# A hybrid attention and gMLP encoder block on one Trainium2 core: squares by tokens, normalisation on VectorE, one-matmul gate scales, mixes of two query tiles in one run, and a re-laid order of steps

## The chip, the cores and the metric

The kernel runs on one core of a Trainium2 chip. The metric is the device time in microseconds (us) of one execution. The engines are TensorE (PE, with its weight loads shown apart as PEld), VectorE (DVE), ScalarE (ACT), GpSimd (POOL) and SyncE (SP). SP's queue issues nearly all DMAs, ACT's queue a few.

## The reference

One pre-norm layer over 1024 tokens of width 1024, then a final RMSNorm. Cut to what matters:

```python
h = rmsnorm(x, norm_gain)
z = h @ w_in                       # 1024 x 4864, split into eight parts
q, k, v, gate_a, u_in, v_in, gate_b, g_merge = split(z)
q, k = axial_rope(rmsnorm(q, q_gain)), axial_rope(rmsnorm(k, k_gain))
attn = softmax(q k' / 8) v * silu(gate_a)        # 8 query heads, 2 key heads of 64
y_a  = attn @ w_proj_attn
vv   = layernorm(gelu(v_in)), mixed by a 128 x 128 matrix per channel group inside chunks of 128 tokens
gm   = gelu(u_in) * (w_spatial vv + b_spatial) * silu(gate_b)
y_b  = gm @ w_proj_gmlp
g    = sigmoid(g_merge + b_merge)                # two gates of width 1024
out  = rmsnorm(x + (g0 * y_a + g1 * y_b) @ w_out, final_gain)
```

## The kernel before, in words

Nearly every product is made three times, as high times high, high times low and low times high part (`mm3`, L187 to L190, and `z_mm`, L568 to L573), in fp32r or fp16. Splitting an operand takes one ACT instruction for the high part and one DVE instruction for the low part (`split16`, L301 to L303; `split`, L122 to L124).

The work goes in stages, and a scheduler keeps roughly to the order in which the program lists the steps (L964 to L1298, written out by hand, with dependences, buffer rings and a few `high_priority` blocks):

1. **Load stage.** x arrives transposed (`xT`, eight tiles of 128 channels x 1024 tokens, `load_x`, L158) with the k/v weights and the v_in weights (`nat_weight`, tile `wraw`, ring of 4). PE makes k and v (tile `kv`) and the first v_in group (tile `v`, `v_group`, L474). For the RMS of each token, `add_square` squares each x tile on ACT (L178, six tiles) or POOL (L176, two tiles), DVE adds the eight squares up (L182), and eight one-column matmuls (L265, tile `sst`) sum over channels. `power_rstd` (L138 to L140; the power is on POOL) makes `rstd`. Eight matmuls (L280, tile `rb`) and two DVE copies (L283) lay it out along the free axis as `rB`.
2. **Norm stage.** `v_group(1)` to `v_group(3)` run on PE; each ends in two Gelu instructions on ACT that empty its bank (L481, tile `vst`). x is read again as four pairs of tiles (`load_pair`, L310, tile `xp`). `norm_part` (L312) multiplies each tile with `rB`: tiles 0, 1 and 3 on DVE (L315), tiles 2, 4, 5, 6 and 7 on POOL as two halves each (L318). `norm_split` (L322) scales and splits them into the fp16 tiles `x16`, on ACT (L302) and DVE (L303). `scales` reads the q weights and four more blocks on ACT's queue (tiles `sqq`, `squ`, ...) for unit scales, and `prep_q` (L508) loads, scales and splits the eight q weight halves (tiles `wraw`, `wq`). `v_post` and `spatial` are the gMLP token mix (tile `sp`), and `bias_term` (L495) its bias: one 512-column matmul with ones and four DVE instructions on 64 rows each.
3. **q stage.** `q_group(0)` to `q_group(3)` on PE (tile `q`), between them `spatial`, key transposes, and the query chain `q_norm`, `q_split` that ends in transposed queries `qT`.
4. **Attention.** 64 `scores` steps (L632), one for each head of a pair, query tile and pair of heads j: four score matmuls, row maximum on DVE (L640), exponential on ACT (L644), the normalised fp16 high part on ACT (L650) and low part on DVE (L651), then a DMA transpose on SP's queue into tile `T` (L654, ring `ptr` of 2). 32 `mix` steps (L656) multiply a transposed tile with v: 48 small matmuls into the one bank `o`, and an ACT copy of 128 columns (L667). 24 fills (`run_fill`, gates and u, 24 matmuls each into the one bank `z`) lie between them, with their weights from `prep_next`.
5. **After attention.** `proj_b` (tile `yb`), eight gate pairs (tile `g`), `proj_a` (tile `y`), the output product (tile `out`) and the final norm. Each gate pair takes a unit scale from `unit_scale` (L287): four matmuls of one column that add up in PSUM (L292, tile `usg`), an ACT copy (L294) and four POOL instructions.

PSUM has three banks of 1024 columns in ring `S` (for `kv`, `v`, `sp`, `q`, `s` and the later stages) and one of 512 each for `o` and `z`. So a `q_group` can start only when an earlier tile in its bank has been emptied.

Of the kernel before, what the change touches and what calls it, by code (L numbers as in the profile page):

```python
# [30 lines left out]
def hybrid_block_kernel(  # L31
# [60 lines left out]
    def C(c):  # L92
        return slice(128 * c, 128 * c + 128)
# [17 lines left out]
    ones = t2("ones")[:, 0:P]  # L111
    dve.memset(ones, 1.0)

# [38 lines left out]
    def load_x(dt):  # L152
        raw = t4("T16", f"xraw{dt}")
        t = tX(f"xhl{dt}")
        hi, lo = t[:, 0, :], t[:, 1, :]
        cuts = [slice(0, 256), slice(256, 512), H(1)] if dt == 0 else [H(0), H(1)] if dt < 3 else [slice(0, 1024)]
        for i, r in enumerate(cuts):
            nc.sync.dma_start(out=raw[:, r], in_=xT[C(dt), r])  # L158
            if dt == 0 and i == 0:
                nc.scalar.dma_start(out=cs, in_=cst[:, 0:C_BSP])  # L160
            if dt == 0 and i != 1:
                first_w(i // 2)
        for r in cuts:
# [5 lines left out]
        xraw0.append(raw)  # L169

    ssq = []

    def add_square(dt):
        t = t4("xa", f"xsq{dt}")
        if dt in SQPOOL:
            pool.tensor_tensor(out=t, in0=xraw0[dt], in1=xraw0[dt], op=ALU.mult)  # L176
        else:
            act.activation(t, xraw0[dt], AF.Square)  # L178
        if dt == 0:
            ssq.append(t)  # L180
        else:
            (pool if dt in ADPOOL else dve).tensor_tensor(out=ssq[0], in0=ssq[0], in1=t, op=ALU.add)  # L182

    xraw0 = []
    SQPOOL, ADPOOL = (1, 4), ()
# [20 lines left out]
    for i in range(4):  # L206
        for j in range(2):
# [49 lines left out]
    dve.tensor_scalar(out=gsc[:, 0:1], in0=ssp[:, 16:17], scalar1=2.0 ** -16, scalar2=1e-30, op0=ALU.mult, op1=ALU.add)  # L257
# [4 lines left out]
    sst = ps_o("sst")  # L262
    for tt in range(NT):
        with tc.high_priority():
            pe.matmul(sst[:, tt:tt + 1], ssq[0][:, C(tt)], ones[:, 0:1], start=(tt == 0), stop=(tt == NT - 1))  # L265
    power_rstd(rstd, sst[:, 0:NT], NT, 1.0 / D)
# [20 lines left out]
    def unit_scale(ss, n, name, tag="sc", bufs=3):  # L287
# [3 lines left out]
        for i in range(n):  # L291
            pe.matmul(pt[:, 0:1], mscale.broadcast_to([P, P]), ss[:, i:i + 1], start=(i == 0), stop=(i == n - 1))  # L292
        sc = sb.tile([P, 2], F32, tag=tag, bufs=bufs, name=f"sc{name}")
        act.copy(sc[:, 1:2], pt[:, 0:1])  # L294
# [10 lines left out]
    x16, xpair = {}, {}  # L305
# [14 lines left out]
    NPD = (0, 1, 3)  # L320

    def norm_split(dt):  # L322
        raw = xpair[dt // 2][:, dt % 2, :]
        if dt < 4:
            t = sb.tile([P, 2, 1024], F16, tag="xa", bufs=BUFS["xa"], name=f"x16{dt}")
        else:
            if dt % 2 == 0:
                x16["t"] = tX16(f"x16{dt}")
            t = x16["t"][:, dt % 2]
        split16(t[:, 0, :], t[:, 1, :], raw, gs[:, dt:dt + 1], "dve")  # L330
        x16[dt] = t
# [163 lines left out]
    def bias_term(h):  # L495
        pt = ps_o(f"wsum{h}")
        pe.matmul(pt, ones, wsr[h], start=True, stop=True)
        for t in (2 * h, 2 * h + 1):
            for g2 in range(2):
                rows = slice(64 * g2, 64 * g2 + 64)  # L500
                dve.scalar_tensor_tensor(
                    out=bsp[rows, C(t)], in0=pt[rows, C(2 * (t % 2) + g2)], scalar=cs[rows, C_LNB + t:C_LNB + t + 1],
                    in1=bsp[rows, C(t)], op0=ALU.mult, op1=ALU.add)
# [128 lines left out]
    def scores(j, qt, h):  # L632
# [331 lines left out]
    v_group(0)  # L964
    bsp = t2("bsp")
# [18 lines left out]
    load_wsp(0)  # L984
    early = scales(["q"] + order[:4], ["xa"] * 8)
# [3 lines left out]
    load_pair(0)  # L989
    norm_part(3)  # L990
    v_group(1)
    ktmp = t4("vS", "ktmp")
    head_norm(kn, ktmp, 0, 8, "kf")
    v_group(2)
# [5 lines left out]
    rope(kn, ktmp, Ak, Bk, 8, 2)  # L1000
    norm_part(0)
    norm_split(0)
    norm_part(1)
# [7 lines left out]
    norm_split(1)  # L1011
    v_group(3)
    norm_part(5)
    bias_term(0)
    with tc.high_priority():
# [14 lines left out]
        dve.tensor_scalar(out=vsc, in0=vsc, scalar1=1.0 / (PSCALE * VSCALE), scalar2=None, op0=ALU.mult)  # L1030
    v_post(0)
    spatial(0)
    v_post(1)
    spatial(1)
    bias_term(1)
    norm_split(3)
    prep_q(0)
    prep_q(1)
    prep_q(2)
    prep_q(3)  # L1040
    dve.tensor_tensor(out=v3, in0=v3, in1=vinv[:, None, :].broadcast_to([P, 8, 128]), op=ALU.mult)
# [19 lines left out]
    norm_split(7)  # L1061
    kT = [tX(f"kT{v}") for v in range(2)]
    khl = tX("khl")
    khl = [khl[:, 0, :], khl[:, 1, :]]
    split(khl[0], khl[1], kn, act)
    q_group(0)
    v_post(3)
    spatial(2)
    qT = [t8("qT", 4, f"qT{j}") for j in range(4)]
    k_transposes(0)  # L1070
    v_post(4)
    k_transposes(1)
    q_norm(0)
    v_post(5)
    k_transposes(2)
    spatial(3)
    scales(order[4:6])
    k_transposes(3)
    q_group(1)
    spatial(5)  # L1080
    prep_next()
    spatial(4)
    q_group(2)
    q_split(0)
    prep_next()
    q_split(1)
    v_post(6)
    spatial(6)
    scales(order[6:8])
    v_post(7)  # L1090
    q_norm(1)
    prep_next()
    q_split(2)
    spatial(7)
    q_group(3)
    prep_next()
    q_split(3)
    v_affine(1)
    v_affine(0)
    scores(*hs[0])  # L1100
    prep_next()
    v_affine(3)
    prep_next()
    scales(order[10:12])
    scores(*hs[1])
    scores(*hs[2])
    scales(order[8:10])
    scores(*hs[3])
    v_affine(2)
    run_fill(*halves[0])  # L1110
    prep_next()
    scores(*hs[4])
    q_norm(2)
    run_fill(*halves[1])
    q_split(5)
    scores(*hs[5])
    scores(*hs[6])
    mix(*hs[0][:2])
    q_split(4)
    scores(*hs[7])  # L1120
    mix(*hs[2][:2])
    scores(*hs[8])
    scores(*hs[9])
    q_norm(3)
    scores(*hs[10])
    scores(*hs[11])
    q_split(6)
    q_split(7)
    mix(*hs[4][:2])
    scores(*hs[12])  # L1130
    scores(*hs[13])
    mix(*hs[6][:2])
    run_fill(*halves[2])
    mix(*hs[8][:2])
    scores(*hs[14])
    scores(*hs[15])
    scores(*hs[16])
    mix(*hs[10][:2])
    scores(*hs[17])
    scores(*hs[18])  # L1140
    mix(*hs[12][:2])
    scores(*hs[19])
    mix(*hs[14][:2])
    run_fill(*halves[3])
    run_fill(*halves[4])
    prep_next()
    prep_next()
    run_fill(*halves[5])
    run_fill(*halves[6])
    scores(*hs[20])  # L1150
    run_fill(*halves[7])
    scores(*hs[21])
    scores(*hs[22])
    mix(*hs[16][:2])
    mix(*hs[18][:2])
    run_fill(*halves[8])
    scores(*hs[23])
    scores(*hs[24])
    prep_next()
    scores(*hs[25])  # L1160
    scores(*hs[26])
    mix(*hs[20][:2])
    run_fill(*halves[9])
    prep_next()
    scores(*hs[27])
    scores(*hs[28])
    scores(*hs[29])
    run_fill(*halves[10])
    mix(*hs[22][:2])
    scores(*hs[30])  # L1170
    mix(*hs[24][:2])
# [3 lines left out]
    run_fill(*halves[11])  # L1175
    scores(*hs[34])
    run_fill(*halves[12])
    mix(*hs[26][:2])
    scores(*hs[35])
    mix(*hs[28][:2])  # L1180
    scores(*hs[36])
    prep_next()
    scores(*hs[37])
    scores(*hs[38])
    mix(*hs[30][:2])
    run_fill(*halves[13])
# [91 lines left out]
    gate(6)  # L1278
    pws[7] = pair_weights(7)
# [3 lines left out]
    split_y(0)  # L1283
# [112 lines left out]
```

## Time and profile before

| | us |
|---|---|
| median of 3 runs | 746.68 |
| lowest and highest | 745.58, 747.12 |
| the profiled execution | 748.41 |
| its span in the trace | 746.6 |
| PE busy in the span | 713.0 (95%) |
| DVE busy | 591.8 (79%) |
| ACT busy | 452.6 (61%) |
| POOL busy | 132.3 (18%) |

A matmul of 512 columns has a duration of about 0.38 to 0.40 us in the trace, but the next one starts some 0.22 us after it, because matmuls overlap. So PE's time is read here from the starts of its matmuls, and its busy share only tells where it stood idle. Times within the span are counted from the span's start.

### The profile page before, as it was taken

What the parts mean: (1) busy time and instruction counts of PE and PEld (TensorE: products, weight loads), DVE (VectorE), ACT (ScalarE), POOL (GpSimd) and SP (SyncE); (2) the same over time, 40 slices, a digit from 0 to 9 for tenths busy, and PEclk for the clock granted to TensorE, in tenths of its full rate; (3) what the DMA queues carried; (4) which work ended last, traced back from release to release, by engine and by line L of the source; (5) the groups of instructions that cost most, each with busy time, mean ns of one, the idle gap of its engine ahead of it and who ended that gap; (6) DMA issues with size and microseconds to landing.
All of it is one profiled execution on the core that took longest, in us unless ns stands there. A gap on an engine that the chain in (4) does not pass through costs nothing.

```text
span 746.6 us, 12013 instructions
## 1 busy us (share of the span) xinstructions
PE 713.0 (95%) x4685; PEld 471.2 (63%) x4685; DVE 591.8 (79%) x824; ACT 452.6 (61%) x808; POOL 132.3 (18%) x118
## 2 busy tenths in 40 slices
PE   7989879889999999999999999999999999999996
PEld 7978636455556555666656787556464466478885
DVE  7859989879989999777977699889687898972323
ACT  8563468887688898677785477655463445531011
POOL 3027731332301020001110025202002010000000
PEclk9999979999999999999999999999999999999999
DMA  8690144437487996998889921130031013330202
GB/s 309 224 356 7 57 140 155 129 113 141 88 176 144 205 196 114 160 164 141 156 150 219 270 85 45 41 127 16 1 141 57 1 56 128 135 137 26 110 32 84
DMA packets 156360, 93.98 MB, mean 126 GB/s; under 512 B 135824, under 2 KB 136464, under 8 KB 156304
## 3 DMA queue, kind: packets, MB, share of 16 engines
q1 hardware_dynamic: 154864, 88.75, 47.4%
q10 hardware_dynamic: 1440, 4.47, 1.7%
q8 instruction: 36, 0.59, 0.3%
q14 instruction: 20, 0.16, 0.1%
HBM read 55.46 MB, written 4.19 MB: 80 GB/s over the span
## 4 chain that ended last, share of the span: by engine, by line
PE 47%; DVE 20%; DMA 11%; ACT 10%; issue 7%; POOL 4%; SPq 1%; POOLq 0%; DVEq 0%; ACTq 0%
DMA T<-p 5%; PE out L189 4%; PE out L190 4%; PE out L188 4%; DVE p L651 4%; DVE nm L640 3%; PE g L188 3%; PE g L190 3%; PE g L189 3%; ACT p L650 2%; DMA sqq<-in_wall_dram 2%; DMA xraw<-in_xT_dram 2%; ACT P L644 2%; PE o L663 1%; DMA wraw<-in_wall_dram 1%
## 5 line engine op out<-in xcount | busy, mean ns | idle before, releaser
L651 DVE SCALAR_TENSOR_TENSOR p<-P,ri,p 128x1024 f16<-128x1024 f32 x64 | 83.4, 1307 | 18.2 <-ACT p L650 17.9
L644 ACT ACTIVATE P<-s,nm 128x1024 f32<-128x1024 f32 x64 | 71.2, 1113 | 27.6 <-DVE nm L640 23.6
L650 ACT ACTIVATE p<-P,ri 128x1024 f16<-128x1024 f32 x64 | 72.8, 1143 | 17.3 <-DVE ri L647 11.6
L640 DVE TENSOR_REDUCE nm<-s 128x1 f32<-128x1024 f32 x64 | 77.4, 1212 | 1.3 <-PE s L638 1.3
L637 PE MATMUL s<-kT,qT 128*128 128x512 f32 x128 | 56.7, 443 | 3.5 <-ACT P L644 2.7
L663 PEld LDWEIGHTS <-vS 128*64 128x64 f16 x1536 | 45.4, 110 | 18.0 <-issue 17.7
L663 PE MATMUL o<-T,vS 128*64 128x128 f16 x1536 | 52.8, 220 | 1.3 <-DMA T<-p 0.9
L638 PE MATMUL s<-kT,qT 128*128 128x512 f32 x128 | 50.8, 397 | 0.0
L923 ACT ACTIVATE sq<-xr 128x1024 f32<-128x1024 f32 x7 | 7.4, 1063 | 63.5 <-DVE xr L1326 63.2
L1326 DVE TENSOR_TENSOR xr<-out,xr 128x1024 f32<-128x1024 f32 x7 | 8.6, 1225 | 45.9 <-PE out L190 45.7
L295 POOL TENSOR_SCALAR scg<-scg 128x1 f32<-128x1 f32 x8 | 7.0, 871 | 190.7 <-ACT scg L294 110.4
L189 PE MATMUL out<-wo,yhl 128*128 128x512 f32 x96 | 37.4, 392 | 0.0
L188 PE MATMUL out<-wo,yhl 128*128 128x512 f32 x96 | 37.3, 392 | 0.0
L190 PE MATMUL out<-wo,yhl 128*128 128x512 f32 x96 | 37.3, 390 | 0.0
L188 PE MATMUL g<-x,wg 128*128 128x512 f16 x96 | 36.4, 379 | 0.0
L189 PE MATMUL g<-x,wg 128*128 128x512 f16 x96 | 36.4, 379 | 0.0
L190 PE MATMUL g<-x,wg 128*128 128x512 f16 x96 | 36.4, 379 | 0.0
L188 PE MATMUL q<-wq,x 128*128 128x512 f16 x64 | 25.5, 398 | 10.1 <-ACT vst L481 7.5
L637 PEld LDWEIGHTS s<-kT,qT 128*128 128x128 f32 x128 | 24.3, 190 | 12.1 <-ACT P L644 3.8
L188 PE MATMUL v<-nh,xhl 128*128 128x512 f32 x64 | 25.8, 403 | 2.5 <-DVE vn L238 2.5
L596 POOL TENSOR_TENSOR vm<-vm,ut 128x512 f32<-128x512 f32 x8 | 13.4, 1675 | 82.7 <-DVE ut L382 42.3
L302 ACT ACTIVATE wg<-graw,scg 128x512 f16<-128x512 f32 x16 | 11.6, 722 | 26.3 <-PE g L190 12.9
(548 smaller groups left out, 2113.4 us busy)
## 6 DMA issues: line engine op xcount, KB each, us to landing
wraw<-in_wall_dram SPq DMA_DIRECT2D x75, 256.0 KB, 3.3
graw<-in_wall_dram SPq DMA_DIRECT2D x16, 512.0 KB, 5.0
xraw<-in_xT_dram SPq DMA_DIRECT2D x13, 512.0 KB, 5.2
xp<-in_xT_dram SPq DMA_DIRECT2D x8, 512.0 KB, 8.7
wor<-in_wall_dram SPq DMA_DIRECT2D x8, 512.0 KB, 4.5
xr<-in_x_dram SPq DMA_DIRECT2D x8, 512.0 KB, 4.4
out_dram<-xr SPq DMA_DIRECT2D x7, 512.0 KB, 2.6
sqq<-in_wall_dram ACTq DMA_DIRECT2D x4, 512.0 KB, 5.8
```

Source lines behind the costliest of these rows:

```text
L188: pe.matmul(o, ah, bh, start=start, stop=False)
L189: pe.matmul(o, ah, bl, start=False, stop=False)
L190: pe.matmul(o, al, bh, start=False, stop=stop)
L302: act.activation(hi, raw, AF.Copy, scale=sc)
L596: pool.tensor_tensor(out=vm[:, et, H(h)], in0=vm[:, et, H(h)], in1=t, op=ALU.mult)
L637: pe.matmul(sp[:, H(hf)], qs, kT[v][:, 0, H(hf)], start=True, stop=False)
L638: pe.matmul(sp[:, H(hf)], qs, kT[v][:, 1, H(hf)], start=False, stop=True)
L640: dve.tensor_reduce(out=nm, in_=sp, axis=AX.X, op=ALU.max, negate=True)
L644: act.activation(Pt, sp, AF.Exp, bias=nm, accum_out=rsum)
L650: act.activation(hi, Pt, AF.Copy, scale=ri)
L651: dve.scalar_tensor_tensor(out=lo, in0=Pt, scalar=ri, in1=hi, op0=ALU.mult, op1=ALU.subtract)
L663: pe.matmul(ot[64 * h:64 * h + 64, 0:128], vS[:, kt, v, 64 * vl:64 * vl + 64], T[:, h, 8 * p + kt, :], start=(n == 0), stop=(n == len(part ...
```

## The change

It has five parts, and with them a new written order of steps.

- **Squares by tokens.** x is read once more, by tokens (eight tiles `xn` of 128 tokens x 1024 channels), and ACT squares each with a running sum into one column of `ssx`. The DVE adds, the POOL squares and the eight `sst` matmuls are gone.
- **Normalisation on VectorE.** `NPD` is now all eight tiles, so `norm_part` is one DVE instruction each, and POOL does none.
- **Gate scales.** `unit_scale` makes one matmul of four columns; ACT's activation sums these four columns as it reads them.
- **Bias term.** Two 256-column matmuls with a half-zero ones tile, and two DVE instructions on 128 rows.
- **Mixes.** `mix2` does two query tiles in one run of 96 matmuls into the two halves of the bank `o`, the later tile first, with one copy of 256 columns. Every third transposed tile lies in ring `X` and no longer in `ptr`, so that three are there in all.

```diff
+    ssx = const([P, NT], "ssx")
+    def add_square(tt):
+        xn = t4("xa", f"xn{tt}")
+        nc.sync.dma_start(out=xn, in_=x[C(tt), :])
+        act.activation(xn, xn, AF.Square, accum_out=ssx[:, tt:tt + 1])
...
+            if dt > 3:
+                add_square(2 * dt - 8)
+                add_square(2 * dt - 7)
...
-    sst = ps_o("sst")
-    for tt in range(NT):
-        with tc.high_priority():
-            pe.matmul(sst[:, tt:tt + 1], ssq[0][:, C(tt)], ones[:, 0:1], start=(tt == 0), stop=(tt == NT - 1))
-    power_rstd(rstd, sst[:, 0:NT], NT, 1.0 / D)
+    power_rstd(rstd, ssx, NT, 1.0 / D)
...
-        for i in range(n):
-            pe.matmul(pt[:, 0:1], mscale.broadcast_to([P, P]), ss[:, i:i + 1], start=(i == 0), stop=(i == n - 1))
+        pe.matmul(pt[:, 0:n], mscale.broadcast_to([P, P]), ss, start=True, stop=True)
         sc = sb.tile([P, 2], F32, tag=tag, bufs=bufs, name=f"sc{name}")
-        act.copy(sc[:, 1:2], pt[:, 0:1])
+        act.activation(pt[:, 8:8 + n], pt[:, 0:n], AF.Copy, accum_out=sc[:, 1:2])
...
-    NPD = (0, 1, 3)
+    NPD = range(8)
...
-        pe.matmul(pt, ones, wsr[h], start=True, stop=True)
+        w4 = wsr[h].rearrange("p (t g i) -> p t g i", t=2, g=2)
+        for g2 in range(2):
+            pe.matmul(pt[:, 0:256], onz[:, 64 * g2:64 * g2 + P], w4[:, :, g2, :], start=(g2 == 0), stop=(g2 == 1))
...
+            tg, nb = (("ptr", 2), ("ptr", 2), ("X", 8))[(8 * j + qt) % len((("ptr", 2), ("ptr", 2), ("X", 8)))]
+            T16[j, qt] = sb.tile([P, 2, 16, 128], F16, tag=tg, bufs=nb, name=f"T{j}{qt}")
...
+    def mix2(j, q0):
+        v = j // 2
+        ot = ps_o(f"o{j}{q0}")
+        parts = [(kt, vl, p) for kt in range(8) for vl, p in ((0, 0), (1, 0), (0, 1))]
+        for k in (1, 0):
+            T = T16[j, q0 + k]
+            for n, (kt, vl, p) in enumerate(parts):
+                for h in range(2):
+                    pe.matmul(ot[64 * h:64 * h + 64, C(k)], vS[:, kt, v, 64 * vl:64 * vl + 64], T[:, h, 8 * p + kt, :],
+                              start=(n == 0), stop=(n == len(parts) - 1))
+        if q0 == 0:
+            og[j] = t4("og", f"og{j}")
+        act.copy(og[j][:, 128 * q0:128 * q0 + 256], ot[:, 0:256])
...
-    mix(*hs[0][:2])
+    mix2(*hs[0][:2])
```

Two places show what the new order does to an engine's rows. The first is SP's queue in the load stage. In the kernel before, the x tiles (`xraw`), weights (`wraw`) and constants (`bsp`, `rtr`, `gq`) follow each other so:

```order
L128 DMA wraw_252<-in_wall_dram 128x512
L158 DMA xraw_257<-in_xT_dram 128x1024
L966 DMA bsp<-in_cst_dram 128x512
L158 DMA xraw_299<-in_xT_dram 128x1024
L128 DMA wraw_262<-in_wall_dram 128x512
L972 DMA rtr<-in_cst_dram 128x1024
L974 DMA gq<-in_cst_dram 128x256
L158 DMA xraw_337<-in_xT_dram 128x1024
```

In the changed kernel the x tiles by tokens (`xn`) stand between them; these are the first four of eight:

```order
L131 DMA wraw_248<-in_wall_dram 128x512
L161 DMA xraw_253<-in_xT_dram 128x1024
L177 DMA xn_292<-in_x_dram 128x1024
L131 DMA wraw_258<-in_wall_dram 128x512
L177 DMA xn_295<-in_x_dram 128x1024
L161 DMA xraw_298<-in_xT_dram 128x1024
L177 DMA xn_333<-in_x_dram 128x1024
L131 DMA wraw_288<-in_wall_dram 128x512
L177 DMA xn_336<-in_x_dram 128x1024
L131 DMA wraw_327<-in_wall_dram 128x512
L161 DMA xraw_339<-in_xT_dram 128x1024
```

So the later `xraw` tiles stand behind up to four more transfers of 512 KB; the other four `xn` tiles follow between the last `xraw` and `wraw` transfers.

The second place is ACT at the end of the norm stage, where `v_709` and `v_731` are the bank of `v_group(3)`, `x_...` the split x tiles and `wq_...` the q weights. Before:

```order
L302 ACTIVATE x_909<-xp_582,gs 128x1024 x2
L302 ACTIVATE wq_867<-wraw_868,s0q 128x512
L302 ACTIVATE wq_867<-wraw_872,s0q 128x512
L302 ACTIVATE x_933<-xp_912,gs 128x1024
L118 CAST khl<-kn 128x1024
L302 ACTIVATE x_933<-xp_912,gs 128x1024
L302 ACTIVATE wq_867<-wraw_876,s0q 128x512
L481 ACTIVATE vst_698<-v_731,rstd 128x512 x2
L302 ACTIVATE wq_867<-wraw_880,s0q 128x512
```

And in the changed kernel:

```order
L121 CAST khl<-kn 128x1024
L292 ACTIVATE x_881<-xp_604,gs 128x1024 x2
L292 ACTIVATE x_888<-xp_867,gs 128x1024
L292 ACTIVATE wq_704<-wraw_705,s0q 128x512
L292 ACTIVATE wq_704<-wraw_793,s0q 128x512
L292 ACTIVATE x_888<-xp_867,gs 128x1024
L471 ACTIVATE vst_697<-v_709,rstd 128x512 x2
L398 COPY vm<-sp_777 64x4x128 x2
L292 ACTIVATE wq_704<-wraw_806,s0q 128x512
L292 ACTIVATE wq_704<-wraw_843,s0q 128x512
```

The Gelu pair that empties the bank of `v_group(3)` stood behind the third q weight half (`wraw_876`); now it stands ahead of it, behind the first two.

More of the change, by code (lines that the diff above doesn't have):

```diff
@@ L110, in hybrid_block_kernel @@
     dve.tensor_copy(identr, ident)
-    ones = t2("ones")[:, 0:P]
+    onz = t2("ones")[:, 0:P + 64]
+    ones = t2("one")[:, 0:P]
     dve.memset(ones, 1.0)
+    dve.memset(onz, 1.0)
+    dve.memset(onz[:, 64:P], 0.0)
     def hi_part(eng, hi, raw):
@@ L964, in hybrid_block_kernel @@
     v_group(0)
+    v_group(1)
+    load_pair(0)
+    load_wsp(0)
     bsp = t2("bsp")
@@ L988, in hybrid_block_kernel @@
     load_pair(2)
[L989 to L994, printed above, removed]
+    early = scales(["q"] + order[:4], ["xa"] * 8)
     with tc.high_priority():
@@ L1060, in hybrid_block_kernel @@
                              op0=ALU.mult, op1=ALU.subtract)
[L1061 to L1065, printed above, removed]
+    norm_split(0)
+    norm_split(6)
+    v_post(2)
+    norm_split(5)
+    prep_next()
     q_group(0)
-    v_post(3)
+    v_post(4)
+    q_norm(0)
+    spatial(3)
     spatial(2)
[L1069 to L1072, printed above, removed]
@@ L1073, in hybrid_block_kernel @@
-    q_norm(0)
+    spatial(4)
     v_post(5)
     k_transposes(2)
-    spatial(3)
-    scales(order[4:6])
+    q_group(1)
+    v_post(7)
+    k_transposes(1)
+    q_norm(1)
     k_transposes(3)
-    q_group(1)
-    spatial(5)
[L1081 to L1094, printed above, removed]
+    bias_term(1)
+    q_split(0)
+    q_split(1)
@@ L1095, in hybrid_block_kernel @@
+    prep_next()
+    spatial(7)
+    scales(order[6:8])
+    q_split(2)
+    spatial(6)
+    prep_next()
+    q_group(2)
+    spatial(5)
     q_group(3)
[L1096 to L1099, printed above, removed]
     scores(*hs[0])
     prep_next()
-    v_affine(3)
-    prep_next()
-    scales(order[10:12])
+    v_affine(2)
+    q_split(3)
     scores(*hs[1])
     scores(*hs[2])
-    scales(order[8:10])
+    prep_next()
     scores(*hs[3])
-    v_affine(2)
-    run_fill(*halves[0])
-    prep_next()
@@ L1131, in hybrid_block_kernel @@
+    mix2(*hs[0][:2])
+    mix2(*hs[4][:2])
+    scales(order[10:12])
+    scales(order[8:10])
+    run_fill(*halves[1])
+    prep_next()
     scores(*hs[13])
-    mix(*hs[6][:2])
-    run_fill(*halves[2])
-    mix(*hs[8][:2])
+    v_affine(0)
     scores(*hs[14])
+    prep_next()
     scores(*hs[15])
     scores(*hs[16])
-    mix(*hs[10][:2])
     scores(*hs[17])
     scores(*hs[18])
-    mix(*hs[12][:2])
+    mix2(*hs[8][:2])
+    prep_next()
+    run_fill(*halves[2])
     scores(*hs[19])
-    mix(*hs[14][:2])
+    scores(*hs[20])
@@ L1167, in hybrid_block_kernel @@
     scores(*hs[29])
+    run_fill(*halves[9])
+    mix2(*hs[20][:2])
     run_fill(*halves[10])
-    mix(*hs[22][:2])
     scores(*hs[30])
-    mix(*hs[24][:2])
+    run_fill(*halves[11])
     scores(*hs[31])
@@ L1278, in hybrid_block_kernel @@
     gate(6)
+    split_y(0)
     pws[7] = pair_weights(7)
```

212 lines of the change are left out of this document (92 added, 120 removed).

## The prediction

> **What bounds the kernel now.** I read the page first, then the busy times by stage (the windows), and at the stage borders the timeline of PE and of whoever released it. The page and the windows (columns: stretch and its length, then busy us of PE, PEld, DVE, ACT and POOL, PE clock, DMA share, GB/s):
>
> ```profile
> PE 713.0 (95%) x4685; PEld 471.2 (63%) x4685; DVE 591.8 (79%) x824; ACT 452.6 (61%) x808; POOL 132.3 (18%) x118
> ```
>
> ```profile
> 0.00:50.85 50.85, 44.38 (x295) 41.15 (x295) 35.15 (x55) 32.66 (x52) 8.55 (x11) 0.97 0.82 286
> 50.85:86.15 35.30, 35.30 (x152) 29.14 (x153) 31.86 (x40) 15.76 (x23) 24.93 (x22) 0.95 0.24 91
> 86.15:97.55 11.40, 3.86 (x27) 3.26 (x26) 11.33 (x14) 5.98 (x9) 8.56 (x6) 0.81 0.23 70
> 97.55:156.76 59.21, 56.66 (x298) 31.80 (x297) 49.66 (x82) 45.92 (x89) 11.97 (x10) 0.95 0.45 146
> 156.76:408.60 251.84, 242.05 (x2317) 148.64 (x2317) 217.11 (x281) 200.32 (x376) 38.71 (x30) 0.99 0.82 153
> 408.60:746.60 338.00, 330.75 (x1602) 217.19 (x1600) 246.73 (x356) 152.00 (x262) 39.64 (x40) 1.00 0.25 84
> ```
>
> The windows are the load stage, v_group(1) to (3), the gap before q_group(0), the q stage, attention, and the rest. PE stands idle openly in one place, 86.15 to 97.55 (3.86 busy of 11.40); DVE is full there and nearly so before it. PE's busy share flatters it elsewhere, since a matmul's duration overlaps the next. The true rate comes from starts, here at one mix run in attention:
>
> ```profile
> 354.74 0.39 PE L637 MATMUL s<-kT,qT 128*128 128x512 f32 x1
> 354.97 0.39 PE L638 MATMUL s<-kT,qT 128*128 128x512 f32 x1
> 355.29 1.53 PE L663 MATMUL o<-T,vS 128*64 128x128 f16 x48
> 356.75 0.50 PE L637 MATMUL s<-kT,qT 128*128 128x512 f32 x1
> ```
>
> A 512-column score matmul takes 0.23 us (354.97 - 354.74), a mix run 1.46 for 48 (0.0304 each), and the way into a run costs 0.32 - 0.23 = 0.09. So whatever leaves PE's list counts fully after 156.76 unless PE waits for something else, while in the first 157 us what counts is who lets PE start.
>
> **The load stage: -3.5 us.** Its end is the start of v_group(1):
>
> ```profile
> 16.55 0.39 PE L189 MATMUL kv<-wl,xhl 128*128 128x256 f32 x1 [2.06 <-DVE wl L124]
> ...
> 18.13 0.42 PE L190 MATMUL kv<-wh,xhl 128*128 128x256 f32 x1
> ...
> 20.91 0.41 PE L189 MATMUL kv<-wl,xhl 128*128 128x256 f32 x1
> ...
> 22.65 0.28 PE L190 MATMUL kv<-wh,xhl 128*128 128x256 f32 x1
> 22.77 0.28 PE L188 MATMUL kv<-wh,xhl 128*128 128x256 f32 x1
> ...
> 37.09 1.84 PE L265 MATMUL sst<-ones,xsq 128*128 128x1 f32 x16
> ...
> 44.54 1.95 PE L280 MATMUL rb<-identr,rstdh 128*128 128x128 f32 x16
> ...
> 50.85 0.47 PE L188 MATMUL v<-nh,xhl 128*128 128x512 f32 x1 [2.51 <-DVE vn L238]
> ```
>
> ```profile
> GB/s 309 224 356 7 57 140 155 129 113 141 88 176 144 205 196 114 160 164 141 156 150 219 270 85 45 41 127 16 1 141 57 1 56 128 135 137 26 110 32 84
> L182 DVE TENSOR_TENSOR xsq<-xsq,xsq 128x1024 f32<-128x1024 f32 x7 | 8.5, 1211 | 0.0
> L178 ACT ACTIVATE xsq<-xraw 128x1024 f32<-128x1024 f32 x6 | 6.3, 1042 | 0.0
> 42.00 1.66 POOL L140 TENSOR_TENSOR rstd<-rstd,mhalf 128x8 f32<-128x8 f32 x1 [23.15 <-DVE rstd L139]
> ```
>
> Gone are 8.5 us of DVE adds and some 1.7 us of PE (the 1.84 at 37.09, overlapping a little); both PE waits above (2.06 and 2.51) are for DVE, so both should go. Added are 8 x 512 KB = 4.19 MB on SP's queue. Slices of 18.7 us moved 309 and 356 GB/s when the queue had work; the transfers that now stand in the order up to the last `xn` are 12.2 MB on SP's queue, and about 1 MB comes on ACT's by then; at 335 GB/s, from 2 us on, they end at 41.5 (an estimate from these). One square (1.04) and the power (1.66) with the small steps around them give `rstd` at about 44.4, where the power ended at 43.66 before. The last v_in weights stand behind the last `xn`: landing 42.3, split 0.7 on ACT and 0.7 on DVE, eight matmuls 1.8, so 45.5, then `rb`, 1.95, and v_group(1) at about 47.4 where it was 50.85. Bounds: all PE terms count (-1.7 -2.06 -2.51, with what the clock loses, below, about -7); or all of 4.19 MB pushes (12.5 us at 335), v_group(1) then at 58 (+7.5). I take -3.5, nearest to the page's two slices.
>
> The first wait has a second price. Behind its 2.06 us the 256-column matmuls from 18.13 to 20.91, 14 by their starts, stand 0.21 apart, where 0.12 is usual (22.65 to 22.77): half rate, 1.3 us lost in 2.8. I expect two such short waits in the new load stage too, for the late weights and for `rstd`, and leave both spells in the sum. The Trainium skill ("TensorE: Matmul & The Clock Gate", Part 1: The HAM clock gate) has the clock halved only after an idle window of about 3.4 us. This trace disagrees, with half rate behind 2.06. By that rule new waits of 2 to 3 us would leave the rate alone, and the sum would be about 1.3 lower for each: 725 to 726.
>
> **q_group(0): another -9.5 us.** The queues at the gap, and PE behind it:
>
> ```profile
> 89.73 0.28 PE L190 MATMUL sp<-wsh,vl 128*128 128x256 f32 x1
> ...
> 97.55 0.59 PE L188 MATMUL q<-wq,x 128*128 128x512 f16 x1 [7.54 <-ACT vst L481]
> ...
> 103.42 0.38 PE L190 MATMUL q<-wq,x 128*128 128x512 f16 x1
> 103.64 0.38 PE L188 MATMUL q<-wq,x 128*128 128x512 f16 x1
> ```
>
> ```profile
> 95.63 0.72 ACT L302 ACTIVATE wq<-wraw,s0q 128x512 f16<-128x512 f32 x1 [4.75 <-DMA wraw<-in_wall_dram]
> 96.26 1.25 ACT L481 ACTIVATE vst<-v,rstd 128x512 f32<-128x512 f32 x2
> ```
>
> PE waited 7.54 us for the bank of v_group(3); its Gelu pair stood on ACT behind a q weight half whose transfer came 4.75 us late. In the new order the pair stands ahead of that half. Then the 14 q matmuls from 97.55 to 103.42 started 0.42 apart where 0.22 follows (103.64 - 103.42): about 2.9 us lost after the idle. Both go: 10.4, of which I keep 0.9 back for waits on q weight transfers, so 9.5. The other thing that q_group(0) needs is `x16`, now all from DVE:
>
> ```profile
> 50.62 1.28 DVE L283 COPY rB<-rb 128x512 f32<-128x512 f32 x2
> 59.37 1.20 DVE L315 TENSOR_TENSOR xp<-xp,rB 128x1024 f32<-128x1024 f32 x1
> L315 DVE TENSOR_TENSOR xp<-xp,rB 128x1024 f32<-128x1024 f32 x3 | 4.6, 1572 | 0.0
> L303 DVE SCALAR_TENSOR_TENSOR x<-xp,gs,x 128x1024 f16<-128x1024 f32 x8 | 12.1, 1530 | 0.1
> L318 POOL TENSOR_TENSOR xp<-xp,rB 128x512 f32<-128x512 f32 x10 | 14.7, 1501 | 7.7 <-DVE rB L283 7.7
> 96.69 1.28 DVE L303 SCALAR_TENSOR_TENSOR x<-xp,gs,x 128x1024 f16<-128x1024 f32 x1
> ```
>
> POOL loses 14.7 us; DVE gains five norms of 1.20 (the fast one, at 59.37) = 6.0. While POOL works on the same tiles DVE's take 1.57 and 1.53 instead of 1.20 and 1.28, so POOL's silence returns 3 x 0.37 + 8 x 0.25 = 3.1. DVE did 31.86 + 11.33 = 43.2 us of work between 50.85 and 97.55; if all of it stays ahead of the last `x16`, with 2.9 more, from `rB` at about 50 it ends at 96. PE, at q_group(0) from about 87 (90.0 less 3.5), asks for tile 7 after 42 matmuls (two token halves of seven tiles, three products each) of 0.22, at 96. So it is just covered, and the new order also puts statistics of `v_post` behind it. If that cover is gone, it costs what rival two says.
>
> **Gate scales: -4.8 us.**
>
> ```profile
> 518.96 0.38 PE L189 MATMUL g2T<-x,wg2T 128*128 128x512 f16 x1
> 519.18 0.95 PE L292 MATMUL usg<-gss,mscale 128*128 128x1 f32 x8
> 519.99 0.38 PE L190 MATMUL g2T<-x,wg2T 128*128 128x512 f16 x1
> ```
>
> Eight records (two for each fp32 matmul) hold PE 0.81 us; two of them leave about 0.2, so 0.6 goes, eight times, in the stage where PE runs without waits. ACT's summing copy takes as long as the plain one to within 0.1 us, far from PE's needs.
>
> **Mixes -1.6, bias 0.** The matmuls of the mixes stay 1536. 16 of 32 run edges go, at 0.09 to 0.1: 1.5 to 1.6; 16 short ACT copies too, beside PE's work. What the pairs do to waits I count at nothing: third buffer and wait for the later tile work against each other (rivals one and five). `bias_term` loses four short DVE instructions in the gap; two 256-column matmuls equal one of 512.
>
> **Sum.** -3.5 -9.5 -4.8 -1.6 = -19.4. The profiled execution had 748.41 for its span of 746.6 and stands 1.7 above the median of 746.68, so 729.0 for it and **727.3** for the median, say 727.
>
> **Rivals.**
> 1. *Attention waits shrink too.* In 156.76 to 408.60 PE's work by distances is 256 score matmuls x 0.23, 1440 of mixes x 0.0304, 552 of 23 fills x 0.22 and some 7 us of transposes: 59 + 44 + 121 + 7 = 231, so some 21 of 251.84 are lost. A third transposed tile lets scores run further ahead, and half as many handovers of bank `o` remain. Two fifths of that loss, 8.5 less: 719. Against: DVE (217.11 of 251.84) stays as full.
> 2. *It does less than it says early: DVE sets the q stage.* DVE is busy 49.66 of 59.21 us there; with PE arriving 13 us earlier, q norms, splits and `x16` catch it up. Some 6 to 7.5 of the 9.5 are handed back: 734. For: both PE waits of the load stage were for DVE, and normalising was moved onto it. Against: net only 2.9 more.
> 3. *The re-read of x holds PE.* `rb` stands ahead of v_group(1) in PE's list, so a late `rstd` stops all matmuls: v_group(1) at 58 instead of 47.4, 10 of the gain lost: 737. For: the DMA share in the load stage is 0.82. Against: the queue had slack at 57 to 75 us (7 GB/s).
> 4. *Slower: pairs wait for the later tile.* A run of 96 begins with the later of two tiles, so no first mix covers that tile's transposition:
>
> ```profile
> T<-p SPq DMA_TRANSPOSE x64, 4.7
> L663 PE MATMUL o<-T,vS 128*64 128x128 f16 x1536 | 52.8, 220 | 1.3 <-DMA T<-p 0.9
> ```
>
> Both buffers come free later, so scores' transpositions queue, and PE stands at 16 runs. Until now waits ahead of mixes cost 1.3 us in all. It turns the result at 19.4 / 16 = 1.2 us a run; at half a transposition (2.4) it is 38: 765. Against: one more buffer, and fills stand around the runs.
>
> **How the numbers follow.** Chances: forecast 0.47 (720 to 732), rival one 0.17, two 0.20, three 0.07, four 0.09. The range of 715 to 740 holds the first four but their tails. 0.2%, 1.5 us, is what can be told from no change; only where rival four ends near its turning point does the time fall there: same 0.04; faster 0.87, slower 0.09.
>
> **What would show it.** Right: v_group(1) at 46 to 49, q_group(0) without idle at 85 to 88 and at full rate, first score near 144, usg at 0.2 us, mix runs of 2.9 us. Wrong: idle before `rb` released by `rstd`; q matmuls waiting for `x` or `q` banks and a first score beyond 150; mix runs preceded by waits for `T`; attention longer than 252 us.

## The result, and the profile after

The changed kernel takes **722.14 us** (median; 720.09 to 723.10) beside 746.18 for the kernel before in the same runs: a ratio of 0.967, 95% interval 0.965 to 0.970. The forecast was 727 in a range of 715 to 740. The profiled execution took 722.31 for a span of 720.5, 26.1 less than the profiled execution before.

The first lines of the page, as before: busy time by engine, then the bytes moved in each of 40 slices.

```profile
PE 696.2 (97%) x4625; PEld 461.9 (64%) x4625; DVE 575.5 (80%) x820; ACT 455.2 (63%) x810; POOL 117.1 (16%) x106
...
GB/s 295 402 405 117 89 132 134 203 37 110 117 136 189 217 183 128 187 187 178 137 202 206 193 102 15 132 72 3 41 106 1 58 88 176 116 118 12 106 30 87
```

PE lost 16.8 us of busy time and still rose to 97%. The core's DMA engines moved 402 and 405 GB/s in the second and third slices (18 us each), where the forecast had worked with 335.

The windows by stage (length, then PE, PEld, DVE, ACT, POOL), this time with attention up to the first gate pair (tile `g`), since the two kernels put their last fills on different sides of `proj_b`; first after, then the last two stages of before:

```profile
0.00:45.28 45.28, 41.26 (x279) 37.88 (x279) 25.91 (x51) 32.93 (x57) 2.96 (x9) 1.00 0.97 360
45.28:78.90 33.62, 33.62 (x155) 28.01 (x154) 32.90 (x43) 22.14 (x32) 11.05 (x9) 1.00 0.44 169
78.90:82.64 3.74, 3.74 (x30) 3.56 (x28) 3.74 (x7) 2.45 (x5) 0.00 (x0) 1.00 0.49 162
82.64:141.47 58.83, 54.31 (x301) 31.27 (x300) 50.86 (x88) 45.96 (x89) 18.20 (x18) 0.99 0.46 150
141.47:441.85 300.38, 291.12 (x2631) 190.53 (x2631) 265.41 (x354) 233.15 (x422) 61.15 (x34) 0.99 0.79 153
441.85:720.50 278.65, 272.12 (x1239) 170.61 (x1238) 196.70 (x283) 118.61 (x209) 23.76 (x36) 0.99 0.21 74
```

```profile
156.76:462.66 305.90, 295.76 (x2637) 190.44 (x2637) 265.06 (x353) 232.53 (x435) 54.88 (x34) 0.99 0.76 151
462.66:746.60 283.94, 277.04 (x1281) 175.39 (x1280) 198.77 (x284) 119.79 (x204) 23.47 (x36) 1.00 0.20 73
```

| stretch | before | after | change | forecast |
|---|---|---|---|---|
| start to v_group(1) | 50.85 | 45.28 | -5.6 | -3.5 |
| v_group(1) to q_group(0) | 46.70 | 37.36 | -9.3 | -9.5 with the next |
| q_group(0) to the first score | 59.21 | 58.83 | -0.4 | |
| first score to first gate pair | 305.90 | 300.38 | -5.5 | -1.6 |
| first gate pair to the end | 283.94 | 278.65 | -5.3 | -4.8 |

PE at the places that the forecast named (start, length, work, and in brackets the idle time and its releaser):

```profile
43.47 2.05 PE L271 MATMUL rb<-identr,rstdh 128*128 128x128 f32 x16 [0.90 <-DVE rstdh L261]
45.28 0.48 PE L182 MATMUL v<-nh,xhl 128*128 128x512 f32 x1
...
82.52 0.27 PE L184 MATMUL sp<-wsh,vl 128*128 128x256 f32 x1
82.64 0.39 PE L182 MATMUL q<-wq,x 128*128 128x512 f16 x1
82.86 0.38 PE L183 MATMUL q<-wq,x 128*128 128x512 f16 x1
...
141.47 0.80 PE L626 MATMUL s<-kT,qT 128*128 128x512 f32 x1 [3.87 <-ACT qT L453]
...
493.31 0.28 PE L282 MATMUL usg<-gss,mscale 128*128 128x4 f32 x2
493.45 0.38 PE L182 MATMUL g2T<-x,wg2T 128*128 128x512 f16 x1
```

`q_group(0)` now follows the last `sp` matmul without a gap and at full rate (82.64 to 82.86). A new wait stands before the first score, 3.87 us, for query copies on ACT. A gate scale holds PE 0.14 us (493.31 to 493.45), where the one that the forecast showed held 0.81.

### The profile page after: what moved, and what is told of

Same layout as the page of the kernel before. It is cut to its first block, busy times and chain, and to the rows that moved or that the text cites. A ratio compares the mean times of both kernels' runs of the same rounds, so it can differ in the third digit from the quotient of the medians.

```text
span 720.5 us, 11891 instructions
## 1 busy us (share of the span) xinstructions
PE 696.2 (97%) x4625; PEld 461.9 (64%) x4625; DVE 575.5 (80%) x820; ACT 455.2 (63%) x810; POOL 117.1 (16%) x106
## 4 chain that ended last, share of the span: by engine, by line
PE 60%; DVE 14%; DMA 11%; ACT 8%; issue 4%; POOL 1%; SPq 1%; POOLq 0%; ACTq 0%; DVEq 0%
PE out L182 4%; PE out L183 4%; PE out L184 4%; DMA wraw<-in_wall_dram 4%; DMA T<-p 3%; DMA xraw<-in_xT_dram 3%; PE o L654 3%; PE g L182 3%; PE g L184 3%; PE g L183 3%; DVE p L640 3%; DVE nm L629 3%; PE s L626 2%; PE s L627 2%; PE yb L182 1%
## 5 line engine op out<-in xcount | busy, mean ns | idle before, releaser
L654 PE MATMUL o<-T,vS 128*64 128x128 f16 x1536 | 49.9, 220 | 3.7 <-DMA T<-p 3.6
L285 POOL TENSOR_SCALAR scg<-scg 128x1 f32<-128x1 f32 x8 | 18.8, 2348 | 181.1 <-ACT usg L284 181.1
L626 PEld LDWEIGHTS s<-kT,qT 128*128 128x128 f32 x128 | 24.8, 194 | 17.2 <-ACT P L633 5.5
L627 PEld LDWEIGHTS s<-kT,qT 128*128 128x128 f32 x128 | 24.9, 195 | 4.5
L182 PE MATMUL yb<-gm,wh 128*128 128x512 f32 x64 | 25.2, 394 | 0.0
L560 PE MATMUL u<-x,wu 128*128 128x512 f16 x64 | 24.3, 380 | 0.9 <-ACT s1b L357 0.6
```

Source lines behind the costliest of these rows:

```text
L182: pe.matmul(o, ah, bh, start=start, stop=False)
L285: pool.tensor_scalar(out=sc[:, 1:2], in0=sc[:, 1:2], scalar1=1.0, scalar2=1e-30, op0=ALU.mult, op1=ALU.add)
L560: pe.matmul(o, wh, x16[dt][:, 0, H(h)], start=(dt == 0), stop=False)
L626: pe.matmul(sp[:, H(hf)], qs, kT[v][:, 0, H(hf)], start=True, stop=False)
L627: pe.matmul(sp[:, H(hf)], qs, kT[v][:, 1, H(hf)], start=False, stop=True)
L654: pe.matmul(ot[64 * h:64 * h + 64, C(k)], vS[:, kt, v, 64 * vl:64 * vl + 64], T[:, h, 8 * p + kt, :], start=(n == 0), stop=(n == len(parts ...
```

## The experiments

Each was timed in several rounds beside the kernel before, which stood at 746.0 to 746.3. Two columns of the table come from each kernel's own trace: when the first score starts, and how long it is from there to the first gate pair. That second stretch holds the same matmuls in every kernel, to within 8 of some 2630.

| kernel | median us | first score at | attention |
|---|---|---|---|
| before | 746.2 | 156.8 | 305.9 |
| b_gelu: Gelu pair first | 749.9 | 158.8 | 304.6 |
| b_npd: normalisation on VectorE | 744.0 | 146.8 | 310.8 |
| b_sq: squares by tokens | 739.3 | 147.3 | 303.2 |
| b_scale: gate scales | 742.0 | 154.7 | 304.9 |
| b_ring3: third transposed tile | 748.0 | 156.5 | 305.9 |
| b_ops: all changed operations but the pairs | 735.5 | 140.4 | 311.3 |
| b_ops_mix2: and the pairs | 739.0 | 139.0 | 317.0 |
| after: and the new written order | 722.1 | 141.5 | 300.4 |
| a_pool: five tiles on POOL again | 730.9 | 148.2 | 301.1 |
| a_ring2: two transposed tiles | 767.9 | 140.7 | 346.6 |
| a_mix1: pairs as two runs | 744.7 | 140.7 | 324.3 |
| a_late: a step moved | 723.0 | 141.4 | 301.3 |
| a_early: squares behind query copies | 727.4 | 137.7 | 309.9 |

### Who held q_group(0)

The forecast's largest term said that the Gelu pair was late because it stood behind a late transfer. **b_gelu** changes that alone in the kernel before:

```diff
+    s0l = const([P, 1], "s0l")
+    act.activation(s0l, vst[7][:, 0:1], AF.Identity, scale=0.0, bias=wsc["q"][0])
     prep_q(2)   # halves 2 and 3 take the scale from s0l, so after the pair
```

> The kernel before, with one edit: the Gelu pair of v_group(3) stands on ACT ahead of the third q weight half (that half's scale now comes through a one-column copy that waits for the pair), all else in the order of before. Theory one (the prediction's step: PE waits at 90.0 to 97.55 because the pair stands behind a late transfer): q_group(0) starts at 90, at full rate, and 7.5 to 10.4 us go, 736 to 739. Theory two (DVE is what is late: the transfer of the third q weight half was itself held until DVE had split the first ones, at 92 to 93, behind tiles that POOL normalises slowly): q_group(0) starts at 90, does 12 matmuls on the two halves that are there, then waits for the third until about 97 to 98; under 3 us go, 743.5 to 746.

Measured: 749.9, ratio 1.005 (1.003 to 1.006): 3.6 us slower, more than either theory allowed. ACT, DVE and PE in b_gelu:

```profile
89.49 1.25 ACT L481 ACTIVATE vst<-v,rstd 128x512 f32<-128x512 f32 x2
...
94.28 0.72 ACT L302 ACTIVATE wq<-wraw,s0l 128x512 f16<-128x512 f32 x1 [3.22 <-DMA wraw<-in_wall_dram]
```

```profile
90.69 1.38 DVE L303 SCALAR_TENSOR_TENSOR wq<-wraw,s0q,wq 128x512 f16<-128x512 f32 x2
...
99.26 1.40 DVE L303 SCALAR_TENSOR_TENSOR wq<-wraw,s0l,wq 128x512 f16<-128x512 f32 x2
```

```profile
90.79 0.38 PE L188 MATMUL q<-wq,x 128*128 128x512 f16 x1 [3.40 <-ACT vst L481]
...
95.52 0.38 PE L188 MATMUL q<-wq,x 128*128 128x512 f16 x1
98.77 0.45 PE L1018 MATMUL vabT<-identr,vscr 128*128 128x128 f32 x1 [2.87 <-DVE bsp L501]
```

The pair is done at 90.7 and q_group(0) starts at 90.79, but then it has two weight halves and stops after 95.52. The third half still comes to ACT at 94.28 and is split on DVE at 99.26 (where before did it at 97.88; the edit put it some instructions later in DVE's order, which is part of the loss). Why it is late stands in the trace of before, in SP's waits from 78 to 100 us:

```profile
SPq L128 <- DVE wq L303: 17.4, 3, 14.2
```

Its transfer could not start until DVE had split the first halves (at 91.99) and freed their buffers. DVE was late there although it hardly waited: from 70 to 92 us it stood idle for 1.2 us. Its instructions were longer while POOL worked on a tile. This one, with 16 columns, ran beside POOL's tile of 70.58 to 73.12 in the kernel before; below it is the same one in b_npd, the next experiment, where POOL has no tiles:

```profile
70.64 1.26 DVE L420 TENSOR_TENSOR kf<-kf,rstd 128x16 f32<-128x16 f32 x1 [0.23 <-POOL kf L140]
```

```profile
68.18 0.18 DVE L420 TENSOR_TENSOR kf<-kf,rstd 128x16 f32<-128x16 f32 x1 [0.92 <-POOL kf L140]
```

What theory two says of the third half holds, and **b_npd** tries the remedy alone:

```diff
-    NPD = (0, 1, 3)
+    NPD = range(8)
```

> The kernel before, with only the normalisation moved: all eight tiles on VectorE, none on POOL (the scheduler then places the Gelu pair ahead of the third q weight half as well). Theory one: no more than the kernel with the pair alone gains, and less by the 2.9 us of work that DVE takes on: 737 to 742. Theory two: with POOL silent DVE's own instructions shorten and its waits for POOL go, so q weights and x tiles come several us earlier; it gains at least 5 us more than the pair alone, 733 to 740, with q_group(0) before 92 and without a wait for the third half.

q_group(0) starts at 88.46 with 1.03 us of idle time, and the first score comes 10 us earlier (146.8). The Gelu pair stands ahead of the third half here too, but b_gelu shows that this alone is not enough. So moving the normalisation does what the forecast expected of the Gelu pair. But the median falls by 2.3 only, less than either theory had (ratio 0.997, 0.996 to 0.998): attention takes 4.9 us more, and this is the first sight of something that comes up again. **a_pool** is the reverse edit, in the changed kernel:

> The changed kernel, with five of the eight tiles normalised on POOL again (tiles 2, 4, 5, 6, 7), written order kept. Theory one (the order of the Gelu pair is what mattered): 0 to 1.5 us slower than the changed kernel, 722 to 724. Theory two (POOL's tiles and what they do to DVE were what was late): q_group(0) or its first matmuls wait for x tiles again and 4 us or more come back, 726 to 732.

730.9, so 8.7 come back. PE, ACT and POOL in a_pool:

```profile
89.20 0.59 PE L182 MATMUL q<-wq,x 128*128 128x512 f16 x1 [5.87 <-ACT vst L471]
```

```profile
84.10 1.15 ACT L292 ACTIVATE x<-xp,gs 128x1024 f16<-128x1024 f32 x1 [3.27 <-POOL xp L308]
87.27 0.72 ACT L292 ACTIVATE wq<-wraw,s0q 128x512 f16<-128x512 f32 x1 [2.03 <-DMA wraw<-in_wall_dram]
87.90 1.25 ACT L471 ACTIVATE vst<-v,rstd 128x512 f32<-128x512 f32 x2
```

```profile
79.52 4.54 POOL L308 TENSOR_TENSOR xp<-xp,rB 128x512 f32<-128x512 f32 x2
```

The whole chain of before is back: ACT waits 3.27 us for a tile from POOL, then 2.03 for a weight transfer, then come the Gelu pair and PE, after 5.87 us. The Gelu pair stands behind the third half again although the written order is that of the changed kernel. So its place followed from POOL's tiles, and by itself (b_gelu) a better place gained nothing.

**b_sq** puts only the squares by tokens into the kernel before (the parts of the change's diff on `add_square`, `ssx` and `sst`):

> The kernel before, with only the squares by tokens (x re-read by tokens, squares summed on ACT, no DVE adds, no POOL squares, no sst matmuls). Theory one (parts add up): v_group(1) starts 4 to 6 us earlier and all that follows shifts by as much, 741 to 743. Rival (the re-read only fills a gap: what sets q_group(0) is DVE and POOL later on): v_group(1) earlier, but the idle time ahead of q_group(0) grows by as much, 745 to 747.

739.3 (ratio 0.991, 0.989 to 0.993), better than theory one: v_group(1) starts at 45.43, 5.4 earlier, q_group(0) at 88.58, 9.0 earlier, and the first score 9.5 earlier. The rival falls, though q_group(0) still waits 5.11 us for its Gelu pair.

### Gate scales

**b_scale** puts only the new `unit_scale` into the kernel before:

> The kernel before, with only the gate scale as one matmul of four columns and a summing copy. The prediction's term: eight times 0.6 us, 4.8 off, 741.4. Rival (the few columns are covered by the queue of weight loads, and the slower POOL steps behind come late to the gate): 0 to 2 off, 744 to 746.

742.0 (ratio 0.994, 0.993 to 0.996): 4.4 off, with an interval of 3.0 to 5.6. The size stands. Its working does not quite: the forecast took one scale, whose eight records stand together and hold PE for 0.81 us, for all eight. From the first gate pair on, before has seven scales; two stand like that, and most records of the others stand in twos between other matmuls, at 0.14 for each two. The seven hold PE 5.0 us together, and 1.0 in the changed kernel. In b_scale the stage from the first gate pair on takes 280.9, 3.1 less than in before.

### Pairs, buffers and the written order

**a_ring2** takes the third transposed tile from the changed kernel:

```diff
-            tg, nb = (("ptr", 2), ("ptr", 2), ("X", 8))[(8 * j + qt) % len((("ptr", 2), ("ptr", 2), ("X", 8)))]
+            tg, nb = "ptr", 2
```

> The changed kernel with two transposed tiles in all and not three. Prediction's view (third buffer and wait for the later tile cancel, attention otherwise unchanged): without it the pairs wait, some 1 to 2 us in each of 16 runs, 735 to 755. Rival (the scores run ahead far enough through P and p16, T is never short): within 1.5 us of the changed kernel, 721 to 724.

767.9: 45.8 slower than the changed kernel, 2.9 for each of 16 runs and more than either expectation. PE's waits for transposed tiles from 141 to 465 us (total, times, longest), in the changed kernel and then in a_ring2, where the line on ACT shows what it does further back, waits for a free p buffer:

```profile
PE o L654 <- DMA T<-p: 3.6, 5, 1.2
```

```profile
PE o L654 <- DMA T<-p: 13.7, 11, 2.6
...
ACT p L639 <- DMA T<-p: 39.0, 20, 3.6
```

This is rival four, at about its price, once the third buffer is gone. Steps also come in another order on PE in a_ring2, so not all of the 45.8 need be waits for tiles. **b_ring3** gives the third buffer to the kernel before, with its single mixes:

> The kernel before with three transposed tiles in place of two, all else as it was (single mixes). Prediction's forecast: the third buffer alone changes nothing, 745 to 748. Its rival one (attention waits shrink with a third buffer): 3 us or more off, 743 or less.

748.0 (ratio 1.003, 1.002 to 1.004): worth nothing without the pairs, rather 2 us worse. **a_mix1** makes each pair of the changed kernel as two runs with a copy each:

```diff
+    def mix_pair(j, q0):
+        mix(j, q0 + 1)
+        mix(j, q0)
```

> The changed kernel with each pair made as two runs of 48 matmuls with a copy of 128 columns each, later tile first, in the same places. Prediction's term: only the run edges come back, 16 times 0.1, 723.5 to 724. Rival (attention lost 4.3 us less in the changed kernel, because half as many handovers of the bank o are left: the second run must wait for the first one's copy): 3 to 8 us come back, 725 to 730.

744.7, 22.6 slower: neither expectation. The scheduler lays the steps of attention differently once the runs are short: scores, fills and the two runs of a pair come in another order on PE. So this is not the price of run edges or of handovers of the bank `o` alone, and those were not separated; ahead of mixes PE waits for a copy out of `o` for 2.0 us in all. ACT's waits for a free p buffer again tell where it went, 4.8 us in the changed kernel and 23.1 in a_mix1:

```profile
ACT p L639 <- DMA T<-p: 4.8, 5, 2.0
```

```profile
ACT p L639 <- DMA T<-p: 23.1, 17, 4.1
```

**b_ops** has all changed operations but the pairs, in the written order of before, and **b_ops_mix2** the pairs too, each where its second mix stood.

> The kernel before with the changed operations but its own written order and its own mixes: squares by tokens, normalisation on VectorE, one-matmul gate scales, bias term on 128 rows. If the parts add up (7.0, 2.4 and 4.4 us as measured alone): 732.5. If normalisation on VectorE is worth as much here as in the changed kernel, where taking it back costs 8.7: 726 to 728. If all parts relieve the same wait (DVE ahead of q_group(0)), less than their sum: 735 to 738. What is left to the changed kernel's 722 is then the mixes and the written order.

> The kernel above with the pair mixes too (three transposed tiles, each pair written where its second single mix stood), so that only the new written order is missing. The prediction's term: 1.6 us below the kernel above. Rival (pairs need scores and fills that are laid around them): 5 us or more above the kernel above, and the written order of the changed kernel is what makes them cheap.

735.5 (ratio 0.987, 0.985 to 0.989) and 739.0 (0.992, 0.989 to 0.995). So the operations give 10.5 together, less than the 13.7 of the three parts that were measured alone (the bias term was not), and in the old order the pairs cost 3.5, with the rival's sign and less than its 5. The first score of b_ops comes at 140.42, 1.05 us before that of the changed kernel: **all of the early gain comes from the operations, none from the new order.** Then b_ops hands 5.4 us back in attention and b_ops_mix2 11.0. The stage in b_ops, then in b_ops_mix2, from first score to first gate pair:

```profile
140.42:451.74 311.32, 295.54 (x2632) 189.19 (x2631) 264.88 (x354) 232.66 (x432) 53.12 (x34) 0.99 0.76 147
```

```profile
139.00:455.95 316.95, 299.64 (x2632) 190.90 (x2630) 268.22 (x357) 234.56 (x420) 54.91 (x34) 0.97 0.73 145
```

The work of DVE and ACT is that of the changed kernel (265.41 and 233.15) to within 3 us; PE stands 15.8 and 17.3 us, where it stands 9.3 in the changed kernel and 10.1 in the kernel before. The written order is what the last 16.9 us (739.0 to 722.1) come from, nearly all in attention (317.0 to 300.4). About half of that is idle time of PE (17.3 to 9.3) and half its busy time for the same matmuls (299.64 to 291.12), with a granted clock of 0.97 and then 0.99. Which steps of the order bring this was not isolated.

### The wait before the first score

**a_late** was to take away the new wait of 3.87 us:

```diff
-    scales(order[6:8])
     q_split(2)
...
     scores(*hs[1])
+    scales(order[6:8])
```

> The changed kernel with one step moved: the unit-scale reading of two weight blocks (eight squares on ACT that wait for their transfers, from 132.3 to 140.9) is written behind the second score and not ahead of the query transposes. In the changed kernel PE waits 3.87 us before the first score for query copies that stand on ACT behind these squares, and then runs some 4.5 us at half rate. If that wait counts to the end: 3.9 and about 2 of the clock go, 716 to 718.5. If attention is bound by the softmax chain anyway, the wait comes back further on: 721 to 723.

723.0, the time of the second expectation but not for its reason: the wait is still there (4.2 us), so these were not the squares that stood in the way. **a_early** takes the right ones, those of the last four weight blocks, by a zero bias that waits for the query copies:

```diff
+    zb = const([P, 1], "zb")
+    act.activation(zb, qT[3][:, 0, 127:128].bitcast(F32), AF.Identity, scale=0.0)
+    scales(order[10:12], zb=zb)
+    scales(order[8:10], zb=zb)
```

> The changed kernel with one wait added on ACT: the eight squares for the unit scales of the last four weight blocks (which the scheduler had put ahead of the query copies, from 132.3 to 140.9) come behind the copies for the first score. The run that was to show this moved another step and left these squares in place. If the first score's wait of 3.9 us and the half rate behind it count to the end: 716 to 718.5. If the softmax chain of attention takes the gain back, as it took back most of the 10 us that normalisation on VectorE alone brought to the first score: 720 to 723.

The first score comes 3.8 us earlier, at 137.65, without a wait. But the kernel takes 727.4, 5.3 us more than the changed one and more than either expectation. The next score then waits 2.05 us for its own copies, with half rate behind it, and attention in a_early is 9.5 us longer:

```profile
142.53 0.52 PE L629 MATMUL s<-kT,qT 128*128 128x512 f32 x1 [2.05 <-ACT qT L456]
...
143.27 0.63 PE L629 MATMUL s<-kT,qT 128*128 128x512 f32 x1
143.70 0.63 PE L630 MATMUL s<-kT,qT 128*128 128x512 f32 x1
```

```profile
137.65:447.57 309.92, 295.74 (x2632) 191.16 (x2631) 267.03 (x355) 236.44 (x432) 54.75 (x34) 0.97 0.78 154
```

The edit also let the scheduler lay fills and scores differently from there on. How much of the 9.5 is the softmax chain and how much this other order stays open. No version here beat the changed kernel.

## Why the prediction was right, and where it was not

The time lies in the range, 5 us below the forecast, with the sign and nearly the size. Part of that is luck, as the steps show:

- **Load stage, -3.5: the mechanism right, the size too small (-5.6).** The DVE adds and `sst` went as said, and so did both waits for DVE, with two of 0.90 us in their place (`kv` at 32.68, `rb` at 43.47). The granted clock is 1.00 in this stage and no longer 0.97, so the two half-rate spells that the forecast kept in its sum did not come; `sst` (1.7), the waits (4.57 less 1.80) and the old spell (1.3) make about 5.8. What made room for it is a mis-sized term, the transfers: at 400 GB/s and not 335 the last square was done at 37.85 and not 42.5, and the power at 39.79 where the forecast had 44.4:

```profile
36.70 1.06 ACT L178 ACTIVATE xn<-xn 128x1024 f32<-128x1024 f32 x1
37.66 0.19 ACT L178 ACTIVATION_READ_ACCUMULATOR xn<-xn 128x1 f32 x1
```

```profile
38.13 1.66 POOL L143 TENSOR_TENSOR rstd<-rstd,mhalf 128x8 f32<-128x8 f32 x1 [28.11 <-DVE rstd L142]
```

  What holds `rb` now (0.90 us) is again DVE, which gets to `rstdh` at 43.26. Rival three, the re-read of x holding PE, did not occur.
- **q_group(0), -9.5: right in sum (-9.3 and -0.4), wrong in its step.** The prediction says "In the new order the pair stands ahead of that half" and then "Both go", the wait and the half rate. b_gelu moved the pair alone and lost 3.6. What the runs showed in its place: DVE was late, slowed beside POOL's tiles, and held the buffers of the weight transfers; the changed operations bring the first score 16.3 us earlier even in the old order (b_ops). The numbers for DVE were good (x splits of 1.27, norms of 1.21 each), but I used them only to show that nothing is lost there:

```profile
L293 DVE SCALAR_TENSOR_TENSOR x<-xp,gs,x 128x1024 f16<-128x1024 f32 x8 | 10.0, 1274 | 0.0
L305 DVE TENSOR_TENSOR xp<-xp,rB 128x1024 f32<-128x1024 f32 x8 | 9.6, 1210 | 0.0
```

  Rival two named the right engine with the wrong sign: DVE did set this stage, and the change relieved it. Against the 2.9 us of half rate that are gone from the q stage stands the new wait of 3.87 before the first score, and the stage is only 0.4 shorter.
- **Gate scales, -4.8: right in size (4.4 alone), with one reading wrong.** A scale of before mostly does not hold PE 0.81 us but less, in pieces. From the first gate pair on the seven scales take 5.0 us before and 1.0 after, so 4.0 of this stage's 5.3 are theirs and 1.3 have another source, which was not looked for.
- **Mixes, -1.6 and "What the pairs do to waits I count at nothing": the step that failed most, though it cost only 4 us here.** Attention is 5.5 shorter. PE's busy time there fell by 4.6 (295.76 to 291.12, in which run edges and half rate are counted) and its idle time by 0.9; which of them the pairs bring was not separated. But the runs show that attention is no constant: the same matmuls took from 300 to 347 us. It is 5.4 us longer than before in b_ops, where it starts 16.3 earlier; the pairs add 5.6 to that in the old order, and the written order takes back 16.6. Whether the earlier start is what lengthens it is not shown: in b_sq it started 9.5 earlier and was 2.7 shorter. I treated the new order as a matter of the norm stage. It did nothing there and all its work in attention.
- **Rivals.** Rival one's time (719) was nearer than the forecast, but in the old order its reasons do not hold: neither the third buffer alone (b_ring3) nor buffer and pairs together (b_ops_mix2) shortened attention. What shortened it came with the written order. Rival four is real without the third buffer (a_ring2).

That the forecast came out nearly right is owed in part to errors that cancelled: operations alone -10.5, pairs in the old order +3.5, and the written order -16.9 make the -24, and my sum had the pairs at -1.6 and the order's work in attention at nothing.

## What to carry to other kernels

When an engine waits behind a late transfer, ask what let that transfer start: here the queue waited for buffers that a third engine had not yet freed, and reordering the waiting engine alone made it worse. Do not carry a gain at the start of a softmax pipeline through to the end: in three kernels here (b_npd, b_ops, a_early) a first score 4 to 16 us earlier was followed by an attention 5 to 10 us longer than without it, though not in b_sq, with 9.5 us. A buffer and a batching can be worth nothing or less alone (+1.9 and, without the buffer, +45.8) and belong in one experiment together with the order that was laid for them.

## What the runs showed of the hardware

Half rate came behind idle times on both sides of the figure that the forecast cited. In a_early, 2.05 us of waiting were followed by 512-column matmuls 0.43 apart (143.27 to 143.70). In the changed kernel 3.87 us before the first score were followed by the same. A wait of 0.9 us before `rb` was followed by full rate (the `v` matmuls after 45.28 are about 0.23 apart):

```profile
45.59 0.39 PE L183 MATMUL v<-nl,xhl 128*128 128x512 f32 x1
45.82 0.39 PE L184 MATMUL v<-nh,xhl 128*128 128x512 f32 x1
...
142.91 0.63 PE L627 MATMUL s<-kT,qT 128*128 128x512 f32 x1
143.34 0.63 PE L626 MATMUL s<-kT,qT 128*128 128x512 f32 x1
```

The length of the wait alone does not decide it. In b_scale the matmuls ran at half rate right behind 2.80 us of idle time, and in a_ring2 at full rate behind 3.15:

```profile
51.15 0.77 PE L188 MATMUL v<-nh,xhl 128*128 128x512 f32 x1 [2.80 <-DVE vn L238]
51.71 0.63 PE L189 MATMUL v<-nl,xhl 128*128 128x512 f32 x1
52.14 0.63 PE L190 MATMUL v<-nh,xhl 128*128 128x512 f32 x1
```

```profile
140.69 0.50 PE L626 MATMUL s<-kT,qT 128*128 128x512 f32 x1 [3.15 <-ACT qT L453]
141.02 0.40 PE L627 MATMUL s<-kT,qT 128*128 128x512 f32 x1
141.25 0.40 PE L626 MATMUL s<-kT,qT 128*128 128x512 f32 x1
```

The forecast's own case is mixed too: behind the 2.06 us in the kernel before, the matmuls from 16.77 to 17.97 still stood 0.12 apart, and half rate began at 18.13; in b_gelu, 2.04 us at the same place were followed by full rate throughout.

The Trainium skill ("TensorE: Matmul & The Clock Gate", Part 1: The HAM clock gate) puts the idle window at about 3.4 us. The rows with 3.87, 3.15 and 0.9 agree with that, those with 2.05 and 2.80 do not.

Traces of the same order differ. b_ring3 and b_scale run the instructions of the kernel before in the same order up to q_group(0). Their waits there are 9.73 and 4.84 us, where the kernel before waited 7.54, but q_group(0) starts at 97.06 and 96.36 beside 97.55, and attention takes 304.9 to 305.9 in all three. So a single profile settles a step of 5 us in a start or in a stage's length, but not one of 1, and the length of one wait settles little.
